# Where the operands of the FFN-up and pool matmuls start inside their SBUF slots

## The chip, the cores and the metric

One NeuronCore of a Trainium2 chip runs the whole program. The metric is the device time of one execution in microseconds, as the median of several executions. The profiled execution is one further execution, with the hardware profiler on.

## The reference

The program computes two transformer blocks on 256 tokens of width 2048, in float32. Only the second block's parts matter here:

```python
pool = multiscale_pool(u, pool_w, pool_scale)          # D_POOL = 1024
m = sigmoid(g_attn) * (attn @ w_attn_o) + sigmoid(g_pool) * (pool @ w_pool_o)
r = r + rmsnorm(m @ w_out, mix_post_g)                 # 272 tokens: 16 meta + 256
h = rmsnorm(r, ffn_pre_g)
a = causal_dwconv(h @ w_ffn_up, conv_w, conv_b)        # 2048 -> 2 * 5632
gate, val = split(a, 2)
r = r + rmsnorm((gelu(gate) * val) @ w_ffn_down, ffn_post_g)
```

`h @ w_ffn_up` is the largest product of the program: 2048 x 11264 weights against 258 token columns (256 tokens and two of history for the convolution).

## The kernel before

Each float32 factor is split into two float32r parts, a high part (the rounded value) and a low part (the rest), and a product takes three matmuls, `mm3`: high weights times high activations (line 258), high weights times low activations (line 259), low weights times high activations (line 260). These three are called a triple below. Each matmul loads its own 128x128 stationary operand (LDWEIGHTS) and streams a moving operand of 256, 258, 272 or 512 columns.

A feature-major product (`fm_chunk`) makes 128 output features: it streams 1024-column weight tiles of eight 128x128 blocks each through a raw tile (`wr`, by DMA on SyncE's queue, line 213), a cast on ScalarE that makes the high part (`wh`, line 223), and a subtraction on VectorE that makes the low part (`wl`, line 224). Then eight triples run with the weights as the stationary and the activations as the moving operand. FFN-up is such a product. `up_first` does the first 512 features (64 triples, eight weight tiles); `up_chunk` does each later chunk of 128 features with 16 triples, 84 times: 40 chunks up to the first half of the FFN (640 triples, "part 0") and 44 in its second half (704 triples, "part 1"). Between the two halves stands the first half of the down product (512-column matmuls). All chunks read the same 16 activation pairs `rg[k]`. The pool's output projection (`pooled`, weights `wpo`) is 16 chunks of eight triples, 128 in all; each stands after two weight tiles of a gate projection of 16 triples. `pool_out` is another 16 triples.

The activations' high and low part lie in one slot of 576 float32 columns, at the two column offsets that a constant `AT_...` gives (`act_pair`). The weights' high and low part lie in slots of 1088 float32 columns in two rings of four, each at the column offset that `W_...` gives (`wpair`). A slot is 2304 or 4352 bytes long, both a multiple of 256, so an offset stands at the same byte position modulo 256 in every slot of its kind. The stages' constants:

```python
AT_H, W_T, W_H = (48, 304), (48, 48), (0, 32)      # first block, input projections
AT_Y, W_Y = (48, 304), (0, 32)                     # first block, output projection
AT_M, W_M, W_Q = (16, 304), (32, 32), (16, 48)     # second block, K/V/u (272 columns); Q and gates (258, from column 14 on)
AT_A, W_A = (46, 318), (48, 0)                     # attention output projection
AT_P, W_P = (16, 288), (48, 0)                     # pool
AT_X, W_X = (16, 304), (16, 48)                    # mixer output projection
AT_F, W_F = (16, 288), (48, 0)                     # FFN-up
```

Of the kernel before, what the change touches and what calls it, by code (L numbers as in the profile page):

```python
# [50 lines left out]
AT_Y, W_Y = (48, 304), (0, 32)  # L51
AT_M, W_M, W_Q = (16, 304), (32, 32), (16, 48)
AT_A, W_A = (46, 318), (48, 0)
AT_P, W_P = (16, 288), (48, 0)
AT_X, W_X = (16, 304), (16, 48)
AT_F, W_F = (16, 288), (48, 0)


VEC = {}
# [1212 lines left out]
```

## Time and profile before

| what | value |
|---|---|
| median of 3 runs | 1953.02 us |
| the three runs | 1948.29, 1953.02, 1953.57 us |
| profiled execution, whole | 1947.45 us |
| its span, first to last instruction | 1945.7 us |
| PE (matmul) busy | 1920.9 us, 99% |
| PE weight load busy | 1794.4 us, 92% |
| VectorE / ScalarE busy | 1303.6 / 968.7 us |
| mean granted TensorE clock | 0.997 |

Matmuls overlap, so a busy PE doesn't say how fast matmuls follow one another. What a stage costs is read from the starts: the time from the first to the last start of one line's matmuls in a window, divided by their number less one, is the time of one triple. In this kernel that number differs between stages whose triples have the same shape.

### The profile page before, as it was taken

What the parts mean: (1) busy time and instruction counts of PE and PEld (TensorE: products, weight loads), DVE (VectorE), ACT (ScalarE), POOL (GpSimd) and SP (SyncE); (2) the same over time, 40 slices, a digit from 0 to 9 for tenths busy, and PEclk for the clock granted to TensorE, in tenths of its full rate; (3) what the DMA queues carried; (4) which work ended last, traced back from release to release, by engine and by line L of the source; (5) the groups of instructions that cost most, each with busy time, mean ns of one, the idle gap of its engine ahead of it and who ended that gap; (6) DMA issues with size and microseconds to landing.
All of it is one profiled execution on the core that took longest, in us unless ns stands there. A gap on an engine that the chain in (4) does not pass through costs nothing.

```text
span 1945.7 us, 34135 instructions
## 1 busy us (share of the span) xinstructions
PE 1920.9 (99%) x13756; PEld 1794.4 (92%) x13756; DVE 1303.6 (67%) x2014; ACT 968.7 (50%) x1516; POOL 21.6 (1%) x26
## 2 busy tenths in 40 slices
PE   8999999999999999999999999999999999999997
PEld 6878888989999999999999998999998899999886
DVE  7889779778675445755557648877764467676555
ACT  3644556566464445544444446655544444445442
POOL 0000001000000000000000000000000000000000
PEclk9999999999999999999999999999999999999999
DMA  9999766758555444555665554665666655555662
GB/s 374 357 328 344 251 215 218 249 182 268 179 166 161 150 145 131 183 183 185 182 186 184 186 185 149 184 188 185 186 192 191 193 181 183 177 182 179 206 188 88
DMA packets 126478, 391.34 MB, mean 201 GB/s; under 512 B 14320, under 2 KB 16752, under 8 KB 126320
## 3 DMA queue, kind: packets, MB, share of 16 engines
q1 hardware_dynamic: 125600, 388.10, 62.6%
q8 instruction: 108, 1.77, 0.4%
q10 hardware_dynamic: 720, 1.06, 0.2%
q14 instruction: 50, 0.41, 0.1%
HBM read 387.01 MB, written 2.10 MB: 200 GB/s over the span
## 4 chain that ended last, share of the span: by engine, by line
PE 96%; DVE 2%; DMA 1%; ACT 1%; issue 0%; SPq 0%; DVEq 0%; ACTq 0%
PE mm L260 29%; PE mm L258 29%; PE mm L259 29%; PE sc L259 1%; DVE junk L388 1%; PE sc L258 1%; PE tp L259 1%; PE tp L260 1%; PE sc L260 1%; PE tp L258 1%; DVE wl L224 1%; DMA wr<-in_w1t_dram 0%; PE tp L671 0%; DMA wn<-in_w1t_dram 0%; ACT wh L223 0%
## 5 line engine op out<-in xcount | busy, mean ns | idle before, releaser
L224 DVE TENSOR_TENSOR wl<-wr,wh 128x1024 fp32r<-128x1024 f32 x631 | 769.6, 1222 | 450.5 <-ACT wh L223 445.3
L223 ACT CAST wh<-wr 128x1024 fp32r<-128x1024 f32 x631 | 659.0, 1047 | 796.0 <-issue 297.3
L258 PE MATMUL mm<-ap,wh 128*128 128x258 f32 (+2 forms) x3552 | 1006.4, 283 | 0.0
L260 PE MATMUL mm<-ap,wl 128*128 128x258 f32 (+2 forms) x3552 | 1002.2, 282 | 2.6 <-DVE wl L224 2.6
L259 PE MATMUL mm<-ap,wh 128*128 128x258 f32 (+2 forms) x3552 | 1002.4, 282 | 0.0
L260 PEld LDWEIGHTS mm<-ap,wl 128*128 128x128 f32 x3552 | 668.9, 188 | 4.0 <-DVE wl L224 3.4
L259 PEld LDWEIGHTS mm<-ap,wh 128*128 128x128 f32 x3552 | 669.6, 189 | 1.4
L258 PEld LDWEIGHTS mm<-ap,wh 128*128 128x128 f32 x3552 | 666.6, 188 | 1.9 <-issue 0.2
L259 PE MATMUL mm<-wl,ap 128*128 128x512 f32 x656 | 256.5, 391 | 0.1
L260 PE MATMUL mm<-wh,ap 128*128 128x512 f32 x656 | 256.2, 391 | 0.0
L258 PE MATMUL mm<-wh,ap 128*128 128x512 f32 x656 | 251.1, 392 | 0.0
L259 PEld LDWEIGHTS mm<-wl,ap 128*128 128x128 f32 x656 | 123.2, 188 | 27.8 <-DVE wl L224 1.5
L260 PEld LDWEIGHTS mm<-wh,ap 128*128 128x128 f32 x656 | 123.2, 188 | 26.3 <-issue 1.0
L258 PEld LDWEIGHTS mm<-wh,ap 128*128 128x128 f32 x656 | 123.1, 188 | 25.7 <-issue 1.0
L388 DVE CUSTOM_DVE_ANT_0 junk<-wr,cB 128x1024 bf16<-128x1024 f32 x96 | 115.8, 1219 | 11.1 <-DMA wr<-in_wada_dram 10.8
L1164 DVE TENSOR_TENSOR ca<-mm,rinv 128x258 f32<-128x258 f32 x84 | 35.7, 426 | 39.0 <-PE mm L260 39.0
L898 DVE TENSOR_TENSOR pj<-mm,rinv 128x258 f32<-128x258 f32 (+1 forms) x64 | 27.7, 432 | 40.8 <-PE mm L260 40.8
L1166 ACT ACTIVATE co<-ca,vec 128x256 f32<-128x256 f32 x88 | 52.2, 598 | 0.0
L1168 DVE SCALAR_TENSOR_TENSOR co<-ca,vec,co 128x256 f32<-128x256 f32 x88 | 42.4, 484 | 2.7
L1167 DVE SCALAR_TENSOR_TENSOR co<-ca,vec,co 128x256 f32<-128x256 f32 x88 | 41.8, 478 | 0.0
L424 DVE TENSOR_TENSOR acc<-mm,acc 128x512 f32<-128x512 f32 x40 | 26.3, 684 | 7.5 <-PE mm L260 7.5
L408 ACT ACTIVATE ap<-xh,mod 128x256 fp32r<-128x256 f32 x16 | 9.6, 602 | 29.8 <-DVE mod L405 29.8
(274 smaller groups left out, 1136.9 us busy)
## 6 DMA issues: line engine op xcount, KB each, us to landing
wr<-in_wup_dram SPq DMA_DIRECT2D x176, 512.0 KB, 3.6
wr<-in_w_dram SPq DMA_DIRECT2D x128, 512.0 KB, 3.6
wr<-in_wada_dram SPq DMA_DIRECT2D x96, 512.0 KB, 5.3
wr<-in_wdn_dram SPq DMA_DIRECT2D x88, 512.0 KB, 3.7
wr<-in_w1t_dram SPq DMA_DIRECT2D x74, 512.0 KB, 5.1
wr<-in_w1z_dram SPq DMA_DIRECT2D x32, 512.0 KB, 4.3
wr<-in_wout_dram SPq DMA_DIRECT2D x32, 512.0 KB, 3.7
wr<-in_wo_dram SPq DMA_DIRECT2D x32, 512.0 KB, 3.6
```

The source lines that it names most:

```text
L223: nc.scalar.copy(h[:, :n], r_[:, :n])
L224: nc.vector.tensor_tensor(lo[:, :n], r_[:, :n], h[:, :n].bitcast(F32), op=ALU.subtract)
L258: nc.tensor.matmul(ps, l[0], r_[0], start=start, stop=False)
L259: nc.tensor.matmul(ps, l[0], r_[1], start=False, stop=False)
L260: nc.tensor.matmul(ps, l[1], r_[0], start=False, stop=stop)
L388: x = nc.vector.tensor_tensor_reduce(junk[hf], w, cB[:, hf, :], 1.0, 0.0, op0=ALU.mult, op1=ALU.add, accum_out=mpart[:, col, hf:hf + 1])
L424: nc.vector.tensor_tensor(d, ps, d, op=ALU.add)
L898: nc.vector.tensor_tensor(t[:, :n], ps[:, :n], rinv[:, off:off + n], op=ALU.mult)
L1164: nc.vector.tensor_tensor(a[:, :TQ], ps[:, :TQ], rinv, op=ALU.mult)
L1166: nc.scalar.activation(o, a[:, 2:TQ], AF.Identity, scale=v("cw", 2 * 88 + ch), bias=v("cb", ch))
L1167: nc.vector.scalar_tensor_tensor(o, a[:, 1:TQ - 1], v("cw", 88 + ch), o, op0=ALU.mult, op1=ALU.add)
L1168: nc.vector.scalar_tensor_tensor(o, a[:, 0:T], v("cw", ch), o, op0=ALU.mult, op1=ALU.add)
```

## The change

Two lines of constants change. The activations of the pool and of the FFN-up product keep the high part at column 16, and the low part moves from column 288 to column 304. The weights of `wpo` and of FFN-up change sides: the high part moves from column 48 to 0, the low part from 0 to 48. No instruction, wait, tile or DMA is added or removed.

```diff
 AT_A, W_A = (46, 318), (48, 0)
-AT_P, W_P = (16, 288), (48, 0)
+AT_P, W_P = (16, 304), (0, 48)
 AT_X, W_X = (16, 304), (16, 48)
-AT_F, W_F = (16, 288), (48, 0)
+AT_F, W_F = (16, 304), (0, 48)
```

The words of the change give the new places as bytes 0 and 128 modulo 256 for the activations and 192 and 128 for the weights. Columns are four bytes wide, so 16 and 304 are bytes 64 and 192 modulo 256 of the slot, and 0 and 48 are bytes 0 and 192; both fit those words if slots start at byte 192 modulo 256. With that start the old places are 0 and 64 for the activations and 128 and 192 for the weights.

## Rows read from the trace of the kernel before

**Rows 1.** The page: span, busy engines, granted clock in 40 slices, engines of the chain.

```profile
span 1945.7 us, 34135 instructions
...
PE 1920.9 (99%) x13756; PEld 1794.4 (92%) x13756; DVE 1303.6 (67%) x2014; ACT 968.7 (50%) x1516; POOL 21.6 (1%) x26
...
PEclk9999999999999999999999999999999999999999
...
PE 96%; DVE 2%; DMA 1%; ACT 1%; issue 0%; SPq 0%; DVEq 0%; ACTq 0%
```

**Rows 2.** Groups by line, 1234 to 1434 us, then 1556 to 1806: busy, mean ns.

```profile
L260 PE MATMUL mm<-ap,wl 128*128 128x258 f32 x567 | 160.3, 283 | 0.0
L258 PE MATMUL mm<-ap,wh 128*128 128x258 f32 x567 | 157.1, 277 | 0.0
L259 PEld LDWEIGHTS mm<-ap,wh 128*128 128x128 f32 x567 | 106.1, 187 | 0.0
...
L258 PE MATMUL mm<-ap,wh 128*128 128x258 f32 x683 | 196.5, 288 | 0.0
L259 PEld LDWEIGHTS mm<-ap,wh 128*128 128x128 f32 x683 | 131.6, 193 | 0.0
```

**Rows 3.** Line 258 by stage: count, duration min/median/max in ns, first and last start.

```profile
L258 PE MATMUL mm<-ap,wh x133: 275/276/277, 500.0 to 544.9; 128*128 128x256 f32 x133
L258 PE MATMUL mm<-ap,wh x59: 284/287/287, 775.1 to 796.7; 128*128 128x272 f32 x59
L258 PE MATMUL mm<-ap,wh x279: 278/282/293, 840.0 to 939.9; 128*128 128x258 f32 x140
L258 PE MATMUL mm<-ap,wh x113: 278/282/283, 961.9 to 1001.8; 128*128 128x258 f32 x113
L258 PE MATMUL mm<-ap,wh x99: 281/282/286, 1045.0 to 1079.9; 128*128 128x258 f32 x99
L258 PE MATMUL mm<-ap,wh x233: 281/282/283, 1087.7 to 1169.7; 128*128 128x258 f32 x117
L258 PE MATMUL mm<-ap,wh x28: 282/288/292, 1220.0 to 1229.9; 128*128 128x258 f32 x28
L258 PE MATMUL mm<-ap,wh x567: 276/277/278, 1234.0 to 1434.0; 128*128 128x258 f32 x189
L258 PE MATMUL mm<-ap,wh x683: 283/284/293, 1555.8 to 1805.9; 128*128 128x258 f32 x171
```

**Rows 4.** Who waited for whom, 1234 to 1434 us: total us, times, longest.

```profile
ACT wh L223 <- issue: 90.3, 66, 1.8
DVE wl L224 <- ACT wh L223: 35.5, 70, 0.9
DVE ca L1164 <- PE mm L260: 14.0, 33, 0.6
```

**Rows 5.** Matmuls in order of time around 1208.9 and 1230.6 us: start, us, line.

```profile
1208.85 0.28 PE L260 MATMUL tp<-ap,wl 128*128 128x258 f32 x1
1208.97 0.28 PE L259 MATMUL mm<-ap,wh 128*128 128x258 f32 x1
...
1230.62 1.04 PE L1204 MATMUL tp<-ident,r 128*128 128x128 f32 x8
1231.41 0.37 PE L258 MATMUL mm<-ap,wh 128*128 128x258 f32 x1
```

**Rows 6.** The forget gate's matmuls with 8 weight columns, first and last of 24.

```profile
573.10 0.29 PE L258 MATMUL mm<-ap,wh 128*8 128x272 f32 x1
...
575.94 0.29 PE L260 MATMUL mm<-ap,wl 128*8 128x272 f32 x1
```

**Rows 7.** Windows of line 258's matmuls, part 0 and part 1: busy, granted clock, DMA.

```profile
1234.00:1434.00 200.00, 156.85 (x567) 107.10 (x567) 1.00 0.61 186
1556.00:1806.00 250.00, 196.13 (x683) 128.49 (x682) 1.00 0.59 181
```

## The prediction, made before the change was run

> **What bounds the kernel now.** I read the page's busy line and its chain first: matmuls fill 99% of the span and 96% of the chain is PE, at a granted clock that stays in the top tenth [rows 1]. So the time is the sum of the matmuls' starting distances, and an edit that adds no instruction can only move the time by changing those distances. Durations don't show them: a 258-column matmul is recorded with 277 to 288 ns [rows 2], but the next one starts long before it ends. So I went to line 258 by stage and divided the stretch between the first and the last start by the count less one [rows 3]. That gives the time of a triple, line by line in that group:
>
> - 500 us, output projection of the first block, 256 columns: 44.9 us / 132 = 340.2 ns
> - 775 us, u projection, 272 columns: 21.6 / 58 = 372.4
> - 840 us, gates and pool projection mixed, 258 columns: 99.9 / 278 = 359.4
> - 962 us, gates alone, 258: 39.9 / 112 = 356.3
> - 1045 us, attention output, 258: 34.9 / 98 = 356.1
> - 1088 us, mixer output, 258: 82.0 / 232 = 353.4
> - 1220 us, FFN-up, first chunks, 258: 9.9 / 27 = 366.7
> - 1234 us, FFN-up, part 0: 200.0 / 566 = 353.4
> - 1556 us, FFN-up, part 1: 250.1 / 682 = 366.7
>
> The reader is to see two things. Triples of one shape take 353.4 to 366.7 ns depending on the stage; in FFN-up even one and the same code with the same byte positions runs at 353.4 in one stretch and at 366.7 in two others. The clock is 1.00 in both stretches, which is the 2.4 GHz level, and the DMA load is about equal [rows 7]. Nothing on PE waits there: only ScalarE and VectorE wait, for the next tile and for PE [rows 4]. And the rate changes without a stall that belongs to the stage: it turns slow where the order of one triple is disturbed (a chunk that begins with line 259 at 1208.97) and fast again after eight transposes [rows 5], then stays as it is for hundreds of triples. I call these two steady patterns the fast and the slow lock. In the slow one LDWEIGHTS is also longer, 193 against 187 ns [rows 2], so something in the reads of the two operands holds up both.
>
> **The change part by part.** It removes and adds nothing; the wait, DMA and queue order stay. The two edits, activations and weights, can't be priced apart from rows of before, so I price the new pair of positions by the nearest stages. Bytes are modulo 256, worked out from the constants with a slot start of 192.
>
> Before, FFN-up has activations at 0 and 64 and weights at 128 and 192. After, it has activations at 0 and 128 and weights at 192 and 128. Three stages already have activations at 0 and 128:
> - mixer output, weights at 0 and 128: 353.4 ns, in one pattern throughout its 82 us
> - u projection, weights at 64 and 64, 272 columns: 372.4 ns, which is 353.2 when scaled by 258/272
> - forget gate, weights from 192 on, of only 8 columns, 272 columns of activations: 2.84 us / 23 = 123.5 ns each [rows 6], so 370.4 a triple, scaled 351.4
>
> So at 0 and 128 three different weight positions, and even a weight load a sixteenth as long, give 351 to 353 ns. I read from it that with these activation places the moving operand sets the rate and the weights' place matters little; that is an inference from three rows, since no stage has weights at 192 and 128. The other pairs of before give the bounds: 366.7 (slow lock, activations 0 and 64) above; below, the 340.2 of the 256-column stage with weights off by an odd multiple of 64 from the activations, scaled by 258/256 to 342.9. I take 353.4, of the stage that shares the activations' places and column count and one weight place.
>
> What that is worth, against the profiled execution:
> - part 1: 704 triples x (366.7 - 353.4) = 704 x 13.3 ns = 9.4 us
> - the first chunks from 1208.97 to 1230.6, 21.6 us or 59 triples: 59 x 13.3 = 0.8 us
> - the other 581 triples of part 0 run at 353.4 already: 0
> - pool projection: a third of the triples at 840 us are its, the others gates; 3 x 359.4 - 2 x 356.3 = 365.6 ns; 128 x (365.6 - 353.4) = 1.6 us
> - `up_first` (64 triples) and `pool_out` (16): `up_first` runs partly behind the norm's work; at most 80 x 13.3 = 1.1 us to either side, taken as 0
>
> Sum 11.8 us on the path, as PE is the path. What is late next: the weight supply. At 353.4 ns a tile of eight triples is used up in 2.83 us. Part 0 already runs at that pace with the same work per chunk, and there ScalarE idles 90.3 us of 200 waiting for nothing but its next issue [rows 4]; so it costs nothing. The profiled 1947.45 us become 1935.7. Its own three runs' median is 5.6 us above the profiled execution, for a reason that one trace can't show (5.6 us is 420 triples at 13.3 ns, so part 0 may have been in the slow lock in them, but it may be elsewhere). I carry the difference over unchanged: 1953.0 - 11.8 = 1941.2 us.
>
> A rule that speaks against all this: the Trainium skill, "SBUF — State Buffer", section "Who interferes with whom", says that PE never waits on anyone, and "TensorE: Matmul & The Clock Gate", Part 2, that the two read ports make the weight load cost the running matmul nothing. By these the bytes' place is worth 0 us. The trace doesn't fit them: 353.4 and 366.7 ns for one instruction sequence at one clock need a wait that they exclude.
>
> **The rivals.**
> 1. No change. The place does nothing, or the new pair has two locks as well and is caught in them as before. For it: the two locks of FFN-up at one position show that position alone doesn't fix the rate. Against: the pool projection, at the old FFN-up positions, also runs slow (365.6), while no stage with activations at 0 and 128 does. Time 1953.0.
> 2. Slow lock throughout, the case on the slower side. The new pair has only the slow pattern, or the first triple behind the transposes at 1231 falls into it. The deciding point is that start: up to the next disturbance the pattern stays. Price: part 0's 581 triples x 13.3 = 7.7 us, pool 128 x 1.1 = 0.1. Time 1953.0 + 7.9 = 1960.9. For it: in before the slow lock holds in three of four entries, and the new weight places 192 and 128 stand at unequal distances from the moving operand. Against: the three stages above.
> 3. The middle level, 356.2, of gates and attention output. Part 1 704 x 10.5 = 7.4, first chunks 0.6, pool 128 x 9.4 = 1.2, part 0 loses 581 x 2.8 = 1.6: 7.6 us less, 1945.4. For it: two stages with different places sit there.
> 4. No loss at all, 342.9. (704 + 59) x 23.8 + 581 x 10.5 + 128 x 22.7 ns = 27.2 us less, 1925.8. For it: the 256-column stages hold it. Against: no 258-column stage does.
>
> **How the numbers follow.** Forecast (one lock at 353.4) 0.44, no change 0.18, slow throughout 0.18, middle level 0.13, no loss 0.07. The prediction is the forecast's 1941.2; its own range is 1934 (if the runs were like the profiled one) to 1944. The range for 8 in 10 has to take in the slow case and leaves out the no-loss case and the far tails: 1933 to 1962. A measurement of this kernel can tell 0.3%, 5.9 us, from no change: faster means below 1947.2. Forecast and no loss are faster, the middle level by little, so I count half of it as the same: 0.44 + 0.07 + 0.06 = 0.57 faster. Same: 0.18 + 0.07 = 0.25. Slower: 0.18.
>
> **What would show it.** After, the starts of line 258 from the transposes to the first down product and in part 1 should both give 353.4 ns a triple, with LDWEIGHTS of line 259 near 187 ns in both, and the mixed stretch of gates and pool should fall from 359.4 to (2 x 356.3 + 353.4) / 3 = 355.3. Stages with unchanged constants should keep their numbers. The forecast is wrong if either part shows 366.7 or another steady number, which then names the rival; the inference on the weights is wrong if part 0 and part 1 differ again.

## The result, and the profile after

| | before | after |
|---|---|---|
| median | 1950.65 us (4 runs, 1947.06 to 1953.57) | 1936.03 us (4 runs, 1934.33 to 1940.20) |
| ratio after / before | | 0.9931, 95% interval 0.991 to 0.9951 |
| profiled execution, whole | 1947.45 us | 1940.20 us |
| its span | 1945.7 us | 1938.5 us |

The ratio is 13.5 us of 1950.65, with an interval from 9.6 to 17.6 us. The executions of the kernel before fall into two groups, near 1947 and near 1953 us (20 and 16 of 36, none between 1948.3 and 1952.7), so its median depends on how many of each there are, while both its traces are of the lower group. The page of the kernel after (span, busy engines, engines of the chain) differs from [rows 1] in little but the span; its chain passes through PE for 93% and not 96%:

```profile
span 1938.5 us, 34135 instructions
...
PE 1911.1 (99%) x13756; PEld 1784.3 (92%) x13756; DVE 1302.8 (67%) x2014; ACT 969.2 (50%) x1516; POOL 21.8 (1%) x26
...
PE 93%; DVE 3%; DMA 2%; ACT 1%; issue 1%; DVEq 0%; ACTq 0%
```

The number of instructions is the same, and their order on every engine too. What changed stands in the view of line 258 by stage (count, duration min/median/max in ns, first and last start in us), the one that answers to [rows 3]:

```profile
L258 PE MATMUL mm<-ap,wh x131: 276/276/276, 500.0 to 544.9; 128*128 128x256 f32 x131
L258 PE MATMUL mm<-ap,wh x60: 284/286/287, 774.8 to 796.8; 128*128 128x272 f32 x60
L258 PE MATMUL mm<-ap,wh x282: 279/282/285, 840.0 to 940.0; 128*128 128x258 f32 x141
L258 PE MATMUL mm<-ap,wh x113: 279/279/282, 963.8 to 1003.7; 128*128 128x258 f32 x113
L258 PE MATMUL mm<-ap,wh x233: 282/282/282, 1090.0 to 1172.0; 128*128 128x258 f32 x117
L258 PE MATMUL mm<-ap,wh x567: 282/282/282, 1235.7 to 1435.7; 128*128 128x258 f32 x189
L258 PE MATMUL mm<-ap,wh x686: 281/282/282, 1557.9 to 1799.9; 128*128 128x258 f32 x172
```

Divide each stretch by the count less one, as before. FFN-up's part 0 is at 200.0 / 566 = 353.4 ns a triple, as it was; part 1 is at 242.0 / 685 = 353.3 in place of 366.7. The mixed stretch of gates and pool at 840 us is at 100.0 / 281 = 355.9 in place of 359.4; the gates alone at 963 us keep 356.3, the mixer output 353.4, the u projection at 774 us 22.0 / 59 = 372.9. (The first row has 131 and not 133 because a few matmul records are missing there.) The duration's spread has gone as well: in part 1 the line went from 283 to 293 ns before, now from 281 to 282.

The groups by line of the two parts answer to [rows 2] (first the window 1236 to 1436 us, then 1558 to 1800; busy us, mean ns):

```profile
L258 PE MATMUL mm<-ap,wh 128*128 128x258 f32 x567 | 159.9, 282 | 0.0
L260 PE MATMUL mm<-ap,wl 128*128 128x258 f32 x567 | 156.5, 276 | 0.0
L259 PEld LDWEIGHTS mm<-ap,wh 128*128 128x128 f32 x566 | 107.0, 189 | 0.0
...
L258 PE MATMUL mm<-ap,wh 128*128 128x258 f32 x686 | 193.5, 282 | 0.0
L259 PEld LDWEIGHTS mm<-ap,wh 128*128 128x128 f32 x686 | 129.7, 189 | 0.0
```

Both parts now run in the same way: 282 ns for line 258, 276 for line 260, 189 for the weight load. That is not the fast pattern of before, which has 277, 283 and 187 [rows 2], though its rate is the same.

Set by landmarks that both traces have (starts of matmuls), the time went here:

| from, to | before | after | difference |
|---|---|---|---|
| start to the first 272-column matmul | 573.1 us | 576.1 us | +3.0 |
| to the last 272-column matmul | 233.8 | 233.9 | +0.1 |
| to the norm behind the mixer (gates, pool, mixer output) | 368.5 | 367.0 | -1.5 |
| to the first down product (FFN-up part 0) | 259.7 | 260.1 | +0.4 |
| to FFN-up part 1 | 119.4 | 119.5 | +0.1 |
| to the second down product (FFN-up part 1) | 258.4 | 249.0 | -9.4 |
| to the last matmul | 122.2 | 122.2 | 0 |

Two of these lines need a word, since nothing in them was touched by the change. The +3.0 us lie ahead of every edited stage, 2.1 us of them ahead of the first product: in this execution the very first small load, `sc`, came late. The row of ScalarE that waits for it (start, us, idle before and releaser):

```profile
4.15 0.21 ACT L355 ACTIVATE sc<-sc 128x16 f32<-128x16 f32 x1 [1.40 <-DMA sc<-in_cT_dram]
```

In the trace of before it started at 2.83. And part 0's +0.4 hides a gain: in the norm's pause the granted clock fell to the lower of its two levels, 1.2 GHz, and stayed there into the first matmuls behind it (windows of 1183 to 1187.4 and 1188 to 1200 us: busy of each engine, granted clock, DMA):

```profile
1183.00:1187.40 4.40, 4.40 (x20) 4.40 (x21) 4.33 (x10) 1.42 (x3) 0.00 (x0) 0.50 0.00 2
1188.00:1200.00 12.00, 11.95 (x97) 11.33 (x96) 10.81 (x18) 7.46 (x12) 0.00 (x0) 1.00 0.42 132
```

The first 24 matmuls of `up_first` took 5.1 us there and 3.5 us in the trace of before, so the dip cost 1.6 us, and part 0 without it gained 1.2. Such a dip is in three of the eleven traces that have the mixer output and this norm unchanged; in the two others it ends 0.7 us or less behind the first matmul, and the first 24 matmuls take 3.5 us. From the first 272-column matmul to the end of the span it is 1372.6 us before and 1362.3 after: 10.3 us, or 11.9 without the dip.

### The profile page after: what moved, and what is told of

Same layout as the page of the kernel before. It is cut to its first block, busy times and chain, and to the rows that moved or that the text cites. A ratio compares the mean times of both kernels' runs of the same rounds, so it can differ in the third digit from the quotient of the medians.

```text
span 1938.5 us, 34135 instructions
## 1 busy us (share of the span) xinstructions
PE 1911.1 (99%) x13756; PEld 1784.3 (92%) x13756; DVE 1302.8 (67%) x2014; ACT 969.2 (50%) x1516; POOL 21.8 (1%) x26
## 4 chain that ended last, share of the span: by engine, by line
PE 93%; DVE 3%; DMA 2%; ACT 1%; issue 1%; DVEq 0%; ACTq 0%
PE mm L259 29%; PE mm L258 28%; PE mm L260 28%; DMA wr<-in_wada_dram 1%; DVE wl L224 1%; DVE junk L388 1%; PE sc L259 1%; PE sc L258 1%; PE sc L260 1%; PE tp L259 1%; PE tp L260 1%; PE tp L258 1%; DMA wr<-in_w1t_dram 0%; PE tp L671 0%; ACT wh L223 0%
## 5 line engine op out<-in xcount | busy, mean ns | idle before, releaser
L260 PE MATMUL mm<-ap,wl 128*128 128x258 f32 (+2 forms) x3552 | 990.6, 279 | 2.6 <-DVE wl L224 2.6
```

The costliest lines, as they stand in the source:

```text
L260: nc.tensor.matmul(ps, l[1], r_[0], start=False, stop=stop)
```

## The experiments

The theory to be tested (A in the expectations): the activations' places at 0 and 128 give the single steady rate of 353 ns, and the weights' place matters little. Its rivals: the weights' places do it (B), or each pair of places has its own rate (C). All places below are bytes modulo 256, high part first, activations before weights. Rates are times of one triple of line 258 to 260. Diffs are against the kernel before unless another is named, and lines that only set up a scan elsewhere are left out.

**One edit alone.** Two kernels, each with half of the change.

```diff
-AT_P, W_P = (16, 288), (48, 0)
+AT_P, W_P = (16, 304), (48, 0)
-AT_F, W_F = (16, 288), (48, 0)
+AT_F, W_F = (16, 304), (48, 0)
```

> Only the activations move (bytes 0 and 128 modulo 256), the weights stay at 128 and 192. Theory A (the activations' places set the rate): a triple of FFN-up takes 353 ns in part 0 and in part 1, as in the changed kernel, and the time falls by about the changed kernel's 13 us. Rival B (the weights' places set it): the kernel keeps the 353.4 / 366.7 split of before, time within 4 us of before. Rival C (the pair counts, each combination has its own rate): a number that is neither, such as 356 or 360 ns; at 356.2 the time falls by 7 to 8 us.

Measured: median 1951.66 us, ratio to before 1.0007 (0.9994 to 1.002). Line 258 in part 0 and part 1:

```profile
L258 PE MATMUL mm<-ap,wh x550: 277/283/283, 1235.8 to 1435.6; 128*128 128x258 f32 x184
L258 PE MATMUL mm<-ap,wh x674: 277/283/283, 1564.8 to 1809.8; 128*128 128x258 f32 x169
```

That is 199.8 / 549 = 363.9 ns in part 0 and 245.0 / 673 = 364.0 in part 1. Part 1 gains 2.7 ns a triple and part 0 loses 10.5: 704 x 2.7 = 1.9 us less and 581 x 10.5 = 6.1 us more. The trace agrees: from the first 272-column matmul to the end it takes 1376.8 us against 1372.6 before, 4.2 us more. The ratio hides this loss, because ten of the 19 executions of before that it rests on are of the group near 1953 us.

```diff
-AT_P, W_P = (16, 288), (48, 0)
+AT_P, W_P = (16, 288), (0, 48)
-AT_F, W_F = (16, 288), (48, 0)
+AT_F, W_F = (16, 288), (0, 48)
```

> Only the weights move (bytes 192 and 128), the activations stay at 0 and 64. Theory A: the two patterns of before remain, part 1 at 366.7 ns a triple, time within 4 us of before. Rival B: 353 ns in both parts, 13 us less. Rival C: another number.

Measured: median 1944.66 us, ratio 0.9973 (0.9959 to 0.9987). Line 258:

```profile
L258 PE MATMUL mm<-ap,wh x556: 281/281/281, 1235.9 to 1435.7; 128*128 128x258 f32 x186
L258 PE MATMUL mm<-ap,wh x682: 281/281/281, 1559.8 to 1804.9; 128*128 128x258 f32 x171
```

199.8 / 555 = 360.0 ns and 245.1 / 681 = 359.9. From the first 272-column matmul to the end this trace takes 1371.0 us, 1.6 us less than before. So theory A has fallen, and B with it: neither edit alone gives 353. By the traces the activations alone cost 4.2 us, the weights alone save 1.6, and both together save 10.3. What counts is the combination (C).

**Is the slow pattern a lottery?** The kernel before, a second time.

> The kernel before once more, for a second trace. If the pattern of a stretch follows from the program alone, part 0 is at 353.4 and part 1 at 366.7 ns a triple again, and the slow pattern begins at the same matmul (the first chunk behind the first 512 features) and ends behind the eight transposes. If it is a lottery per execution, at least one of the three entries differs, and the runs of before, 1947 to 1954 us, differ by this.

Line 258 in part 0 and part 1 of this execution (1946.82 us):

```profile
L258 PE MATMUL mm<-ap,wh x567: 277/277/277, 1233.7 to 1433.7; 128*128 128x258 f32 x189
L258 PE MATMUL mm<-ap,wh x682: 283/288/292, 1555.9 to 1805.6; 128*128 128x258 f32 x171
```

353.4 and 249.7 / 681 = 366.7 again, and the first chunks run at 366.7 up to the eight transposes as before. In these two traces the patterns follow from the program. They don't say what makes its executions differ: both are of the lower group (1947.45 and 1946.82 us), and no execution of the group near 1953 us was traced.

**What chooses between the two patterns.** The places of before, and eight transposes of a finished down-product tile ahead of part 1:

```diff
     for part in range(NHALF):
+        if part == 1:
+            for hf in range(2):
+                t = ps_t()
+                for q in range(4):
+                    nc.tensor.transpose(t[:, q * P:q * P + P], ffa[hf, 2][:, q * P:q * P + P], ident)
```

> The places of before; eight transposes more stand ahead of part 1's first chunk, and the eight that stood in part 0 at 1231 us move to the end of part 1 with their order. If a disturbance at the entry chooses between the two patterns and the pattern then holds, part 0 stays at 366.7 ns a triple for all its chunks (7.7 us more) and part 1 enters anew, at 353.4 ns if it falls as part 0 did behind its transposes (9.4 us less). If the patterns belong to the parts (to slots, to other engines' work), part 0 runs at 353.4 and part 1 at 366.7 as before.

The transposes stand where they were meant to (matmuls in order of time), and the two parts have changed sides:

```profile
1560.96 0.40 PE L260 MATMUL mm<-wh,ap 128*128 128x512 f32 x1
1561.19 1.04 PE L1216 MATMUL tp<-ident,ffa 128*128 128x128 f32 x8
1561.98 0.37 PE L258 MATMUL mm<-ap,wh 128*128 128x258 f32 x1
```

```profile
L258 PE MATMUL mm<-ap,wh x595: 283/292/292, 1221.9 to 1439.7; 128*128 128x258 f32 x199
L258 PE MATMUL mm<-ap,wh x694: 277/277/277, 1564.9 to 1809.8; 128*128 128x258 f32 x174
```

Part 0, which has lost its transposes, stays at 217.8 / 594 = 366.7 ns to its end; part 1 is at 244.9 / 693 = 353.4. One microsecond of other matmuls at the entry decides about the 9 us behind it. With these places the kernel has two steady patterns, and the entry (what runs on PE just ahead of a stretch) picks one.

**The new places entered in another way.** The same eight transposes in the changed kernel.

> The changed kernel with the same eight transposes ahead of part 1 as in the run that swapped the two patterns of before, so both parts are entered another way. If the new places have one steady pattern, both parts stay at 353.3 ns a triple and the time changes by the transposes alone, about 1 us. If they have a slower second pattern that the entry can choose, one of the parts moves to 356 ns or more, which at 3.3 ns a triple is 2 us for 600 to 700 triples.

```profile
L258 PE MATMUL mm<-ap,wh x590: 282/282/282, 1221.9 to 1430.0; 128*128 128x258 f32 x197
L258 PE MATMUL mm<-ap,wh x691: 282/282/282, 1555.9 to 1799.7; 128*128 128x258 f32 x173
```

208.1 / 589 = 353.3 and 243.8 / 690 = 353.3: both parts as before, in an execution of 1936.20 us. From every entry tried the new places fall into the same pattern.

**All pairs of the weights' places.** Four kernels, each with one of the 16 possible pairs of the activations' places; FFN-up's chunk takes the weights' places by its number, five chunks for each of 16 pairs (the last four of the 84 chunks have the first pair again):

```diff
+SCAN = [(h, l) for h in (0, 16, 32, 48) for l in (0, 16, 32, 48)]
 ...
-        return fm_chunk([(i["wup"][ch, 0], 8), (i["wup"][ch, 1], 8)], rg, TQ, at_w=W_F)
+        at = SCAN[(2 * (j - 2) + e) // 5 % 16]
+        return fm_chunk([(i["wup"][ch, 0], 8), (i["wup"][ch, 1], 8)], rg, TQ, at_w=at)
```

> FFN-up's activations at bytes 0 and 128; its weights take all 16 pairs of 0, 64, 128, 192 in turn, five chunks of 16 triples each, so each pair has its own rate in one trace. Same scan in the mixer output (one chunk each), the gates and K, V, u keep to the scan as well (two chunks or one each). Theory C (the pair of places counts): 353.3 ns with weights at 192 and 128 and at 0 and 128, 364 with 128 and 192, and other rates elsewhere, among them perhaps one below 353. Narrower theory D (only the distance from the moving operand to the weights loaded meanwhile counts): pairs with equal distances have equal rates here and in the scan with activations at 0 and 64. Theory A, refuted by the single edits, would have given 353 nearly everywhere.

> The same scan with FFN-up's activations at 0 and 64, as before. Theory C: 360 ns with weights at 192 and 128, 353.4 or 366.7 with 128 and 192, others elsewhere. Theory D: in mm3 the second matmul streams the low activations while the low weights load, the first and the third stream the high activations while high weights load; with weights 64 further in the second place the distances equal those of the scan with 0 and 128 shifted by 64 in the low weights, so 192 and 64 here should run as 192 and 128 there (353.3) and 128 and 128 here as 128 and 192 there (364).

> FFN-up's activations at bytes 192 and 128, weights through all 16 pairs, five chunks each; K, V and u scan as well, one chunk of 16 triples per pair. Theory E (the rate follows from the places, with 353.3 ns as the least that a 258-column triple reaches): a table of 16 numbers between 353 and 373, each a steady one over its five chunks. If a pair runs below 353, the change has not found the best place. For K, V and u (272 columns) the places of now give 373.3; a lower number at another pair names what is left there, 384 triples.

> Activations at 64 and 128, weights through all 16 pairs. These are the places of the scan with 0 and 64, all shifted by 64. Theory F (only the distances among the four places count, not where they stand): the table equals that scan's when the weights are shifted by 64 too, so 64 and 64 gives 366.6 as 0 and 0 did, 192 and 64 gives 373.3 as 128 and 0 did, 0 and 128 gives 355 as 192 and 64 did. If the places themselves count, the tables differ by more than the 2 ns between chunks of one pair.

The rate of each pair in ns, worked out from the starts of the matmuls as the last eight triples of a chunk, median of the five chunks (the five agree within about 1 ns but where a range stands; each pair but the first was entered only from the pair above it):

| weights | act. 0, 128 | act. 0, 64 | act. 192, 128 | act. 64, 128 |
|---|---|---|---|---|
| 192, 192 | 360.0 | 356.6 | 360.0 | 366.7 and 360.0 |
| 192, 0 | 360.0 | 356.6 | 361.2 to 363.5 | 366.6 |
| 192, 64 | 359.9 | 355.0 to 356.4 | 360.0 | 373.3 |
| 192, 128 | **353.4** | 360.0 | 365.0 | 373.4 |
| 0, 192 | 359.9 | 366.6 | 357.6 | 360.0 |
| 0, 0 | 356.6 | 366.6 | 366.6 | 356.6 |
| 0, 64 | 360.0 | 363.4 | 360.0 | 360.0 |
| 0, 128 | 358.7 to 361.5 | 360.0 | 365.9 to 367.3 | 355.1 to 356.4 |
| 64, 192 | 360.0 | 366.6 | 365.0 | 366.6 |
| 64, 0 | 361.5 | 360.0 | 360.6 to 362.0 | **353.4** |
| 64, 64 | 360.0 | 360.0 | 363.4 | 366.6 |
| 64, 128 | 356.8 | 363.4 | 363.4 | 363.4 |
| 128, 192 | 363.1 to 365.1 | 366.6 | 366.6 | 366.6 |
| 128, 0 | 364.2 to 365.9 | 373.3 | 373.4 | 366.6 |
| 128, 64 | 360.0 | 373.4 | 355.2 | 360.0 |
| 128, 128 | 365.5 to 367.2 | 366.6 | 366.6 | 360.0 |

Line 258 stands one line lower in the first two of these kernels. Its rows for three pairs with activations at 0 and 128 (weights 192 and 128, 0 and 128, 128 and 192):

```profile
L259 PE MATMUL mm<-ap,wh x78: 281/282/283, 1297.7 to 1324.9; 128*128 128x258 f32 x78
L259 PE MATMUL mm<-ap,wh x79: 276/282/289, 1411.8 to 1439.9; 128*128 128x258 f32 x79
L259 PE MATMUL mm<-ap,wh x78: 277/283/284, 1675.7 to 1703.8; 128*128 128x258 f32 x78
```

27.2 / 77 = 353, 28.1 / 78 = 360 and 28.1 / 77 = 365 ns. With activations at 0 and 64, weights 128 and 0, the slowest pair, 28.0 / 75 = 373 ns:

```profile
L259 PE MATMUL mm<-ap,wh x76: 292/292/292, 1705.9 to 1733.9; 128*128 128x258 f32 x76
```

And with activations at 64 and 128, weights 64 and 0, 27.2 / 77 = 353 ns:

```profile
L258 PE MATMUL mm<-ap,wh x78: 283/283/283, 1589.8 to 1617.0; 128*128 128x258 f32 x78
```

What follows. Theory C holds in part: which rates are possible goes by the pair, and they differ by up to 20 ns between pairs. In these scans the change's pair is the only one of the 16 beside its activation places at 353, and none of all 64 is below it. The first scan puts the same 16 weight places through the mixer output, whose activations also stand at 0 and 128, one chunk each: 353.4 with 192 and 128, 356.6 with 0 and 0, 364 with 128 and 192, and all but one of the 16 agree with FFN-up's within about 1 ns (128 and 64 gave 363.7 in place of 360.0). So a rate doesn't belong to the stage.

But the old places are not the only ones with two rates. With activations at 64 and 128 and weights at 192 and 192 the first two chunks and the next two differ, and the fifth is like the first, with the norm's matmuls and the eight transposes between them:

```profile
L258 PE MATMUL mm<-ap,wh x22: 281/286/292, 1209.2 to 1216.9; 128*128 128x258 f32 x22
L258 PE MATMUL mm<-ap,wh x31: 280/280/280, 1218.5 to 1229.3; 128*128 128x258 f32 x31
L258 PE MATMUL mm<-ap,wh x16: 281/286/292, 1230.9 to 1236.4; 128*128 128x258 f32 x16
```

That is 7.7 / 21 = 366.7, 10.8 / 30 = 360.0 and 5.5 / 15 = 366.7 ns. And the mixer output's own places, weights at 0 and 128, hold 353.4 through the whole stage in the traces of before and after, but run at 5.4 / 15 = 360.0 in the first scan's mixer, where the chunk ahead has other places:

```profile
L259 PE MATMUL mm<-ap,wh x16: 276/282/289, 1125.7 to 1131.1; 128*128 128x258 f32 x16
```

So a number of the table is the rate of a pair behind one entry, and another entry may give another. For the change's pair every entry tried in FFN-up and in the scanned mixer gave 353.3 or 353.4.

The two narrower theories do worse. Only distances between the streamed and the loaded operand (D): predicted 353.3 for activations 0 and 64 with weights 192 and 64, which gave 355 to 356, and 364 for 128 and 128, which gave 366.6; the order is right, the numbers are not. Only distances among all four places (F): shifted by 64, the second and the fourth column agree in 12 of 16 pairs; one of the four that don't, 366.6 at (0, 192) against 353.4 at (64, 0), differs by just the 13.3 ns between the two patterns of before, and another by the 6.6 ns between the two rates above, so entry may explain them. That was not tried. K, V and u ran in the third scan at 373 to 378 ns in the chunks without a stall, over all 16 pairs: their present 373.3 is about the least there.

**Are the two odd columns the cause?** FFN-up's later chunks at the places of before with 256 streamed columns in place of 258 (the lines that set the two missing columns to zero are left out here):

```diff
-        return fm_chunk([(i["wup"][ch, 0], 8), (i["wup"][ch, 1], 8)], rg, TQ, at_w=W_F)
+        return fm_chunk([(i["wup"][ch, 0], 8), (i["wup"][ch, 1], 8)], rg, T, at_w=W_F)
```

> The places of before, but FFN-up's later chunks stream 256 columns in place of 258; the convolution's last two columns are set to zero, so the last two tokens are wrong. If the two columns over a multiple of 256 bytes times four make the loss, a triple takes 340 ns in both parts (0.8 per cent less than 342.9 for the columns left out), and 1344 triples give about 27 us less than before. If the places alone make it, the triple stays at 351 to 364 ns and the two patterns remain.

```profile
L258 PE MATMUL mm<-ap,wh x558: 278/283/288, 1235.7 to 1435.8; 128*128 128x256 f32 x186
L258 PE MATMUL mm<-ap,wh x692: 278/283/288, 1559.8 to 1808.0; 128*128 128x256 f32 x173
```

200.1 / 557 = 359.2 and 248.2 / 691 = 359.2 ns. With two columns less part 0 is even slower than with 258 (353.4). So 256 columns alone don't free a product of the loss, and the first block's 340.2 [rows 3] must have another reason beside its column count; that it is its places is likely and not shown. A kernel with those places in FFN-up (activations both at 128, weights at 192 and 64) gave no result: with 258 columns from column 48 on, the high part would run into the low part at column 304. With 256 columns the two parts, whose patterns differ with 258, ran at one rate.

**What is left.** In the first scan's gates, weights at 128 and 0 ran at 353.3 ns where the kernel has 0 and 128 at 356.6. The changed kernel with that:

```diff
-AT_M, W_M, W_Q = (16, 304), (32, 32), (16, 48)
+AT_M, W_M, W_Q = (16, 304), (32, 32), (48, 16)
```

> The changed kernel with the weights of Q and the gates at bytes 128 and 0 in place of 0 and 128; in the scan's gates this pair ran at 353.3 ns a triple, the present one at 356.6. If the scan holds: 512 gate triples x 3.3 ns = 1.7 us less than the changed kernel, Q's 128 triples unknown, some 0.2 to 0.4 us either way; ratio to before about 0.992 against 0.9931 of the change. If the entry between gate and pool chunks brings another pattern, 356.6 or more and no gain.

Measured: median 1934.47 us (1933.56 to 1935.43), ratio to before 0.9926 (0.9909 to 0.9944). Line 258 in the gates alone, then in the stretch mixed with the pool:

```profile
L258 PE MATMUL mm<-ap,wh x114: 280/280/280, 959.8 to 999.8; 128*128 128x258 f32 x114
L258 PE MATMUL mm<-ap,wh x282: 280/282/287, 840.0 to 939.9; 128*128 128x258 f32 x141
```

40.0 / 113 = 354.0 in place of 356.3 ns, and 99.9 / 281 = 355.5 in place of 355.9. From the last 272-column matmul to the norm it takes 366.2 us against 367.0 in the changed kernel: 0.8 us, half of what was expected, because in the mixed stretch the first eight triples behind each pool chunk run at 359.6 before the pattern settles. It is the fastest kernel here, but its interval can't be told from the change's; only the trace says that the step is real.

## Why the prediction was right, and where it wasn't

- **The bound.** Right. The time is the sum of the starting distances, and the saved time lies where they changed: part 1 and the pool.
- **Part 1, 704 triples x 13.3 = 9.4 us.** Measured 9.4 (258.4 to 249.0 us). **Pool, 1.6 us.** Measured 1.5 up to the norm. **First chunks, 0.8 us.** The whole of part 0 gained 1.2 when the clock's dip is left out; the slow first chunks are gone, and the row at 1220 us of [rows 3] has no counterpart. **Weight supply at no cost.** Right: part 1 runs at part 0's pace.
- **The step that failed is the reason for 353.4.** I inferred from three stages that with activations at 0 and 128 the weights' place matters little. The activations alone gave 364 ns and cost 4.2 us in the trace, and the scan has 353 to 367 ns at those places. The stage from which I took the number carries it over only in part: its own weights, 0 and 128, hold 353.4 there with one pair throughout, but ran at 360.0 in the same stage behind another pair and at 358.7 to 361.5 in FFN-up. The number was right because the new pair happens to have it: the size was luck. The same argument gives the activation edit alone 11.8 us less, where the trace shows 4.2 more.
- **Where the inference left its rows.** Two of the three rows were of 272 columns. There the weights' place does matter little: over all 16 pairs K, V and u ran at 373 to 378 ns. Scaling them to 258 columns hid that at 258 the 16 pairs spread over 14 ns. The 8-column weight load showed that 272 columns take 370 ns with little to load; it didn't show that a full load is harmless at every place.
- **The signs.** Both parts at 353.4 came true. The mixed stretch was to fall to 355.3 and came at 355.9. LDWEIGHTS of line 259 was to be near 187 ns and came at 189 in both parts, as the new pair's pattern is not the old fast one.
- **The rivals.** "No change" assumed two patterns at the new places; entered from the down product, from transposes and from other pairs they showed one. "Slow throughout" is what a neighbouring pair does (364 with the activations alone), by its places and not by the start from which I let it be decided. The middle level is where the gates stay. "No loss" was not found in 64 pairs, which cover four of the 16 pairs of activation places; those of the first block are not among them.
- **The total.** 11.8 us forecast, 13.5 measured with 9.6 to 17.6; the traces account for 10.3 between the first 272-column matmul and the end, 11.9 without the dip. Carrying the 5.6 us between median and profiled execution over unchanged was a guess, and it failed: 1941.2 was forecast and 1936.0 measured, while 1935.7 is the forecast without it. The 5.6 us are not noise around one time: they belong to the upper of the two groups of before, about 7 us above the lower. My thought that part 0 was in the slow pattern in those executions (7.7 us by the prediction's count) fits the distance, and the ten executions each of the two half changes, with one rate in both parts, spread over only 3.1 and 1.6 us. But no execution of the upper group was traced, so its cause stays open. Of after's four executions the slowest, 1940.20 us, is the traced one; the late first load and the clock dip, 3.0 and 1.6 us against the trace of before, fit its distance to the other three, 3.5 to 5.9 us.
- **The rule against the change.** By the Trainium skill ("SBUF — State Buffer", section "Who interferes with whom") PE never waits on anyone, a rule about engines that share ports. Here one sequence of instructions at one clock takes 353 to 373 ns by the places of its operands, so for these float32r products the places can't be called free on the strength of that rule. Whether PE's own two reads meet, or a read meets the access of another engine, the runs can't show.

## What to carry to other kernels

Read the starting distances of back-to-back matmuls by stage, not their durations: stages of one shape that run at different steady rates are time to be had without touching an instruction. Choose the places of both operands together and measure them in one run, with the place changed from chunk to chunk; nothing simpler than the whole pair predicted the rate here. Then run the chosen pair alone and from several entries, because a scan shows it behind one entry only. Prefer a pair that keeps its rate from every entry, since with another one an unrelated microsecond of work ahead of a loop can cost 9 us behind it. And look at the single times before taking a median: a kernel whose times fall into two groups has to be traced in both.

## What the runs showed of the hardware that I had not expected

- A pattern, once entered, held through 44 chunks (704 triples), and came back to within a tenth of a nanosecond in a second execution. Two more sets of places showed two rates each, 366.7 and 360.0, and 353.4 and 360.0, by what ran ahead.
- Most steady rates of 258-column triples stand on a ladder: 353.3, 356.6, 360.0, 363.4, 366.6 and 373.4 ns, that is steps of 3.3 or 6.7 ns. What is counted in these steps stays open.
- 256 columns at the places of before take 359.2 ns, more than 258 columns in their fast pattern, 353.4.
- Behind the norm's pause TensorE ran its matmuls at the lower clock level in the trace of after, 0.50 from 1183 to 1187.4 us, at the cost of 1.6 us; in the same place of the trace of before it was at 1.00.
